# A transformer block's expert layer: results fetched beside the last quad's weights, the last quad's wide passes added by one-hot, the first quad's tokens gathered

## The chip, the cores and the metric

The program runs on one core of a Trainium2 chip. The time is the device time of one execution in microseconds (us), the median of several runs. Lower is better.

## The reference

Two transformer blocks run one after the other on 512 tokens of width 1024, all in fp32. The first ends with a mixture of experts, and only that part is changed:

```python
# t: 512 x 1024; 32 experts in 4 groups of 8; top 2 experts of one group per token
combine = sum(one_hot(expert_ids, 32) * w_top[..., None], axis=1)
for e in range(32):
    hid = silu(t @ w_gate[e]) * (t @ w_up[e])        # 1024 -> 256
    out = out + combine[:, e:e + 1] * (hid @ w_down[e])   # 256 -> 1024
x = x + gate2 * out
```

Every token picks a group, then two experts of it, so 1024 (token, expert) pairs are spread unevenly: with these inputs, one group takes most of them.

## The kernel before

The residual `x` is kept transposed (eight tiles `x[k]` of 128 features x 512 tokens). The expert layer (`moe`, from L1047) routes, then works through the experts in eight **quads**: quad q holds expert q of each of the four groups (`ex(q, c)` = 8c + q). Each expert has 32 slots in its quad's tile of 128 rows; what an expert has beyond 32 tokens goes through a **wide pass** of 128 rows (`more`, a runtime `If` on the expert's count, and `wide_pass`). In the traced run the second expert of each quad has such a pass, the other three skip theirs. A further block (L1446) for experts with more than 160 tokens is skipped whole.

Per quad: `expert1` (gate and up, 64 matmuls of 32-row strips, then tanh on ACT and products on DVE), `xpose` of the next quad's tokens (eight transposes, evictions by DVE and ACT in turns), `turn` (transpose of the hidden tile), `expert2` (down projection, 32 matmuls, scaled by ACT), `scatter` of the rows to a DRAM table `yd` by POOL; then the four `If`s with `load(6)` (six weight tiles of 512 KB on SP) and `gather_wide` (POOL, tokens of the wide passes from a DRAM copy `h2d`) after each.

How tokens reach a quad: `fill_table` scatters token numbers and weights to a DRAM table by eight POOL instructions, and ACT loads them back as slot tables (`slots0`, `slots[1]`). Quads 2 to 7 gather by `slots0`. Quads 0 and 1 come too early for that: `select` builds a one-hot `oh` (rank equals slot) and reads token number, weight and target row with 16 small matmuls against `val`. Quad 1 then gathers by that number; quad 0 uses the one-hot itself: `pick` multiplies it with the token tiles `xn` by 64 matmuls.

The last quad (`late` in `expert2`) isn't scattered: its rows are split in two fp32r parts `ys`, and `combine` adds them to `x` by one-hot matmuls, in two halves of 256 tokens. The other results come back from `yd`: `fetch(i)` loads two tiles of 128 rows on SP, `collect(i)` sums them on POOL, transposes, and adds to `x` on DVE. The order at the end:

```python
again = [self.mwt() for _ in range(6)]
...                                  # the block for over 160 tokens (L1446)
got = [fetch(i) for i in range(4)]
ys = expert2(NQ - 1, hT, *gat[NQ - 1][1:3])
for hf, hs in enumerate(HALVES):
    combine(ys, hs)
    for i in (2 * hf, 2 * hf + 1):
        collect(i, got[i])
```

The framework orders each engine's instructions within a stretch between two `If`s by its own estimate of when they are ready, program order deciding among the ready ones; an engine then runs its list strictly in order. `mwt()` hands out 30 weight buffers in rotation. Behind the layer, the second block enters (`enter`): sums of squares (ACT, POOL), four weight tiles split in two fp32r parts (`wsplit`, L257 on ACT, L258 on DVE), then a dense stream of matmuls to the end.

Of the kernel before, what the change touches and what calls it, by code (L numbers as in the profile page):

```python
# [205 lines left out]
class Net:  # L206
# [840 lines left out]
    def moe(self):  # L1047
# [37 lines left out]
        def sm(shape, tag):  # L1085
            return self.t(mp, shape, "r_" + tag)
# [74 lines left out]
        wa = sm([P, 4, NE], "wa")  # L1161
        outer(wa, o1)

        td = sm([P, 4, 2, 4], "td")
        tu = td.bitcast(U32)
        slot = sm([P, 4, NE], "slot")
# [9 lines left out]
        for a, sa in enumerate((s12, s2)):  # L1176
# [2 lines left out]
            v.tensor_scalar_add(tu[:, :, a, 1], tokb, BIG - 1.0 + a * S)  # L1179
            v.tensor_copy(td[:, :, a, 2:3], (w1, w2)[a])  # L1180
            v.tensor_scalar_add(td[:, :, a, 3], tokb, BIG)

        val = sm([P, 4, NE, 3], "val")
        v.tensor_copy(val[:, :, :, 0], tokb.unsqueeze(2).to_broadcast([P, 4, NE]))
        v.tensor_copy(val[:, :, :, 1], wa)
        v.scalar_tensor_tensor(val[:, :, :, 2], a2, float(S), tokb.unsqueeze(2).to_broadcast([P, 4, NE]), op0=ALU.mult, op1=ALU.add)


        q1, q2, q3, q4 = (self.t(self.tp, [P, S], "cy" if q < 2 else "th") for q in range(4))

# [26 lines left out]
        def select(q):  # L1217

            oh = self.t(mp, [P, 4, 4, first], "oh")
            for i in range(4):  # L1220
                v.tensor_tensor(oh[:, i], iota[:, :first].unsqueeze(1).to_broadcast([P, 4, first]),
                                rank[:, i, q::8].unsqueeze(2).to_broadcast([P, 4, first]), ALU.is_equal)
            pv = self.pst([P, 3], "mm")
            for i in range(4):
                for c in range(4):
                    cs = slice(32 * c, 32 * c + 32)
                    mm(pv[cs, :], oh[:, i, c, :], val[:, i, ex(q, c), :], start=i == 0, stop=i == 3, tile_position=(0, 32 * c))
            idx = self.t(mp, [P, 1], "idy", U32, bufs=2)
            v.tensor_scalar_add(idx, pv[:, 2:3], BIG - 1.0)
            wv = self.t(mp, [P, 1], "wv", bufs=2)  # L1230
            v.tensor_copy(wv, pv[:, 1:2])
            return oh, idx, wv, pv

        def fetch_tokens(xg, idu):
            g_.indirect_dma_start(out=xg, out_offset=None, in_=h2d, in_offset=bass.IndirectOffsetOnAxis(ap=idu, axis=0),
# [1 line left out]

        def gather(q):

            if q == 1:  # L1240
                _, idx, wv, pv = select(q)
                idu = self.t(mp, [P, 1], "idu", U32)
                v.tensor_scalar_add(idu, pv[:, 0:1], BIG - 1.0)
            else:
                at = slots0[:, q, :].bitcast(U32)
                idu, wv = at[:, 0:1], slots0[:, q, 2:3]
                idx = at[:, 1:2] if q < NQ - 1 else slots0[:, q, 3:4]
            fetch_tokens(xg, idu[:, 0:1])
            return xg, idx, wv

        def gather_wide(e, r=1):

            fetch_tokens(oxg[e // 8], slots[r][:, e, 0:1].bitcast(U32))

        def feed(xTs, hf, pt):

            for k in range(4):
                kk = 4 * hf + k
                if k % 2:
                    s.activation(xTs[hf][:, k, :], pt[:, k, :], AF.Identity, scale=self.gs2[:, kk:kk + 1], bias=mod[:, 3, kk:kk + 1])  # L1260
                else:
                    v.tensor_scalar(xTs[hf][:, k, :], pt[:, k, :], self.gs2[:, kk:kk + 1], mod[:, 3, kk:kk + 1], op0=ALU.mult, op1=ALU.add)

        def xtiles():
            return [self.t(mp, [P, 4, P], f"xgT{hf}") for hf in range(2)]
# [7 lines left out]
                feed(xTs, hf, pt)  # L1273
            return xTs

        def pick(oh):

            xTs = xtiles()
            for hf in range(2):
                pt = self.pst([P, 4, P], "mm")  # L1280
                for k in range(4):
                    kk = 4 * hf + k
                    for i in range(4):
                        mm(pt[:, k, :], xn[i][:, kk * P:(kk + 1) * P], oh[:, i].rearrange("p a b -> p (a b)"),
                           start=k + i == 0, stop=k + i == 6)
                feed(xTs, hf, pt)
            return xTs

        def glu(th, gate, up):

            s.activation(th, gate, AF.Tanh, scale=0.5)  # L1291
# [24 lines left out]
            g_.indirect_dma_start(out=yd, out_offset=bass.IndirectOffsetOnAxis(ap=idx, axis=0), in_=y,  # L1316
                                  in_offset=None, bounds_check=2 * S - 1, oob_is_err=False)

        def expert2(q, hT, idx, wv):

            late = q == NQ - 1
            ys = yt[:1]
            if late:
                ys = [self.t(mp, [P, D], f"ys{i}", F32R) for i in range(2)]
                ys.append(self.t(self.tp, [P, S], "sq", F32R))
                v.tensor_scalar(ys[-1], tokens, idx, None, op0=ALU.is_equal)
            for n in range(2):
                py = self.pst([P, S], "mm")
                ns = slice(n * S, (n + 1) * S)
                for k in range(2):  # L1330
                    for c in range(4):
                        cs = slice(32 * c, 32 * c + 32)
                        mm(py[cs, :], hT[:, k, cs], wt[ex(q, c), 4 + k][:, ns], start=k == 0, stop=k == 1, tile_position=(0, 32 * c))  # L1333
                s.activation(ys[0][:, ns], py, AF.Copy, scale=wv)
                if late:
                    v.scalar_tensor_tensor(ys[1][:, ns], py, wv, ys[0][:, ns], op0=ALU.mult, op1=ALU.subtract)
            if not late:
                scatter(ys[0], idx[:, 0:1])
            return ys

        def wide_pass(e, r, w):

            xT = xpose(oxg[e // 8], oxT)
            pt = None
            for a in range(2):
                ps = self.pst([P, 2, P], "mm")
                for k in range(KT):
                    mm(ps.rearrange("p a b -> p (a b)"), xT[k // 4][:, k % 4, :], piece(w, k)[:, 256 * a:256 * a + 256],
                       start=k == 0, stop=k == KT - 1)
                    if a and k == 4:  # L1350
                        pt = self.pst([P, P], "mm")
                        pe.transpose(pt, oth[:, 0, :], ident)
                        s.copy(ohT[:, 0, :], pt)
                glu(oth[:, a, :], ps[:, 0, :], ps[:, 1, :])
            py = [self.pst([P, S], "mm") for _ in range(2)]
            for k in range(2):
                if k:
                    pt = self.pst([P, P], "mm")
                    pe.transpose(pt, oth[:, 1, :], ident)
                    s.copy(ohT[:, 1, :], pt)  # L1360
                for n in range(2):
                    mm(py[n], ohT[:, k, :], w[4 + k][:, n * S:(n + 1) * S], start=k == 0, stop=k == 1)
            for n in range(2):
                s.activation(yt[1][:, n * S:(n + 1) * S], py[n], AF.Copy, scale=slots[r][:, e, 2:3])
            scatter(yt[1], slots[r][:, e, 1:2].bitcast(U32))

        def combine(ys, hs):
# [10 lines left out]
            for i in [ex(q, c) for c in range(4)]:  # L1378
                rvs[i] = nc.values_load(cmi[0:1, i:i + 1], min_val=0, max_val=S)

        def more(e):

            with tc.If(rvs[e] > first):
                wide_pass(e, 1, [wt[e, j] for j in range(6)])

        def rest(e, w, r=2):

# [6 lines left out]
                    wide_pass(e, r, w)  # L1394
                    rest(e, w, r + 1)

        def fetch(i):

            ys = [self.mwt() for _ in range(2)]
            for a in range(2):  # L1400
                nc.sync.dma_start(ys[a], yd[a * S + i * P:a * S + (i + 1) * P, :])
            return ys

        def collect(i, ys):
# [9 lines left out]
                    xs = self.x[kk][:, i * P:(i + 1) * P]  # L1414
                    v.scalar_tensor_tensor(xs, pt[:, k, :], mod[:, 5, kk:kk + 1], xs, op0=ALU.mult, op1=ALU.add)

        gat = {0: select(0)}
        xt = pick(gat[0][0])
        gat[1] = gather(1)
        fill_table()  # L1420
        count(0)
        for c in range(4):
            gather_wide(ex(0, c))
        for q in range(NQ):
            last = q == NQ - 1
            th = expert1(q, xt)

            if not last:
                with tc.issue_after(self.end1.ins):
                    xt = xpose(gat[q + 1][0])  # L1430
                count(q + 1)
            with tc.issue_after(self.end1.ins):
                hT = turn(th)
            if not last:
                if q + 2 < NQ:
                    gat[q + 2] = gather(q + 2)
                with tc.issue_after(self.turned.ins):
                    expert2(q, hT, *gat[q][1:3])
            for c in range(4):
                more(ex(q, c))  # L1440
                load(6)
                if not last:
                    gather_wide(ex(q + 1, c))
        again = [self.mwt() for _ in range(6)]
        top = nc.values_load(cmi[0:1, NE:NE + 1], min_val=0, max_val=S)
        with tc.If(top > first + wide):  # L1446
            for r in range(2, 5):
                wide_slots(g_, r)
            for e in range(NE):
                rvs[e] = nc.values_load(cmi[0:1, e:e + 1], min_val=0, max_val=S)  # L1450
                rest(e, again)
        got = [fetch(i) for i in range(4)]
        ys = expert2(NQ - 1, hT, *gat[NQ - 1][1:3])
        for hf, hs in enumerate(HALVES):
            combine(ys, hs)
            for i in (2 * hf, 2 * hf + 1):
                collect(i, got[i])
        for k in range(KT):
            self.save(f"x2_{k}", self.x[k])

# [512 lines left out]
```

## Time and profile before

| | us |
|---|---|
| median of 3 runs (range) | 2174.67 (2170.82 to 2176.73) |
| the profiled execution: its time | 2174.14 |
| its span, first to last instruction | 2172.3 |
| TensorE busy in the span | 2001.5 |
| mean granted TensorE clock | 0.974 |

The span is what the trace covers; its times count from its first instruction. TensorE (PE) is the matmul engine, with its weight loads on a row of their own (PEld); DVE, ACT and POOL are the vector, scalar and GpSimd engines; SP issues transfers. A "q" behind an engine (ACTq, PEq) is its sequencer, which also issues that engine's transfers. The expert layer lies between about 466 and 809 us of the span.

### The profile page before, as it was taken

The page shows a single profiled execution, that of the slowest core. Times are in us where ns is not written, and L with a number is a line of the kernel's source. Part 1 is how long each engine was busy: PE and PEld are TensorE (multiplying, and loading weights), DVE is VectorE, ACT ScalarE, POOL GpSimd, SP SyncE. Part 2 cuts the span into 40 slices and gives each one's busy share as a digit, 9 for nine tenths or more (in the row PEclk, how much of TensorE's full clock was granted, in tenths as well). Part 3 has the DMA queues.
Part 4 walks back from the last instruction along what each step waited for, and adds up shares of the span by engine and source line. Part 5 has one row for each costly group of instructions (what it writes and reads, how often), then busy time and mean ns, then how long its engine had stood idle before and what let it go on. Part 6 is the DMA issues. An engine that isn't in the chain of part 4 may idle for free. (4 is left out here: it accounts for less than half of the span.)

```text
span 2172.3 us, 32065 instructions
## 1 busy us (share of the span) xinstructions
PE 2001.5 (92%) x12818; PEld 1549.5 (71%) x12818; DVE 1030.4 (47%) x1889; ACT 703.1 (32%) x1173; POOL 218.6 (10%) x243
## 2 busy tenths in 40 slices
PE   5999999778787769999999999999999999999996
PEld 3677767554434348888888788888878888888885
DVE  4763664641111046552455674645664457542443
ACT  3532343122222123322233352524543243322231
POOL 3020002012121121000003200000000041000002
PEclk9999999889999989999999999999999999999998
DMA  8443215366999943333333132423233322333321
GB/s 268 118 137 109 88 52 182 129 241 208 359 394 375 342 172 102 97 90 104 97 97 98 56 100 78 117 65 106 68 104 91 111 68 88 97 95 100 97 88 39
DMA packets 110620, 294.81 MB, mean 136 GB/s; under 512 B 20023, under 2 KB 31415, under 8 KB 110444
## 3 DMA queue, kind: packets, MB, share of 16 engines
q1 hardware_dynamic: 99676, 275.98, 38.9%
q0 software_dynamic: 9856, 14.29, 2.1%
q8 instruction: 113, 1.85, 0.3%
q10 hardware_dynamic: 912, 2.18, 0.3%
q14 instruction: 63, 0.52, 0.1%
HBM read 296.20 MB, written 18.43 MB: 145 GB/s over the span
## 5 line engine op out<-in xcount | busy, mean ns | idle before, releaser
L274 PE MATMUL mm<-xh,wh 128*128 128x512 f32 (+1 forms) x1584 | 615.1, 390 | 10.2 <-ACT wh L257 6.1
L275 PE MATMUL mm<-xl,wh 128*128 128x512 f32 (+1 forms) x1584 | 604.6, 382 | 5.4 <-DVE xl L1578 5.3
L276 PE MATMUL mm<-xh,wl 128*128 128x512 f32 (+1 forms) x1584 | 601.4, 380 | 0.0
L257 ACT ACTIVATE wh<-wraw 128x1024 fp32r<-128x1024 f32 (+3 forms) x282 | 274.1, 974 | 735.7 <-PE mm L275 647.0
L258 DVE TENSOR_TENSOR wl<-wraw,wh 128x1024 fp32r<-128x1024 f32 (+3 forms) x282 | 315.0, 1118 | 192.0 <-ACT wh L257 190.3
L274 PEld LDWEIGHTS mm<-xh,wh 128*128 128x128 f32 x1584 | 301.2, 191 | 76.6 <-ACT wh L257 8.1
L275 PEld LDWEIGHTS mm<-xl,wh 128*128 128x128 f32 x1584 | 302.7, 191 | 60.9 <-DVE xl L1578 7.0
L276 PEld LDWEIGHTS mm<-xh,wl 128*128 128x128 f32 x1584 | 301.6, 190 | 56.8 <-issue 2.0
L340 POOL TENSOR_TENSOR ss<-ss,sq 128x256 f32<-128x256 f32 (+1 forms) x69 | 65.4, 947 | 919.1 <-ACT sq L339 917.4
L274 PE MATMUL mm<-hh,wh 128*128 128x512 f32 (+1 forms) x416 | 148.5, 357 | 0.0
L276 PE MATMUL mm<-hh,wl 128*128 128x512 f32 (+1 forms) x416 | 148.3, 357 | 0.0
L275 PE MATMUL mm<-hl,wh 128*128 128x512 f32 (+1 forms) x416 | 148.2, 356 | 0.0
L1301 PE MATMUL mm<-wmoe,xgT 128*32 128x512 f32 x512 | 68.9, 624 | 21.7 <-DMA wmoe<-in_wmoe 11.6
L276 PEld LDWEIGHTS mm<-hh,wl 128*128 128x128 f32 x416 | 78.6, 189 | 11.3
L274 PEld LDWEIGHTS mm<-hh,wh 128*128 128x128 f32 x416 | 78.6, 189 | 11.3
L275 PEld LDWEIGHTS mm<-hl,wh 128*128 128x128 f32 x416 | 78.6, 189 | 11.3
L1638 DVE TENSOR_TENSOR sq<-mm,rsb 128x512 f32<-128x512 f32 x44 | 30.4, 691 | 104.0 <-PE mm L276 103.8
L1333 PE MATMUL mm<-wmoe,hT 128*32 128x512 f32 x256 | 51.9, 624 | 24.9 <-DMA wmoe<-in_wmoe 14.2
L1633 DVE TENSOR_TENSOR cy<-mm,rsb 128x512 f32<-128x512 f32 x44 | 30.4, 690 | 85.4 <-PE mm L276 83.5
L1301 PEld LDWEIGHTS mm<-wmoe,xgT 128*32 128x32 f32 x512 | 20.5, 114 | 67.9 <-issue 34.0
L1292 DVE SCALAR_TENSOR_TENSOR mth<-mth,mm 128x256 f32<-128x256 f32 x8 | 3.4, 420 | 114.5 <-ACT mth L1291 88.7
L1333 PEld LDWEIGHTS mm<-wmoe,hT 128*32 128x32 f32 x256 | 11.8, 113 | 60.2 <-issue 29.0
(510 smaller groups left out, 2587.0 us busy)
## 6 DMA issues: line engine op xcount, KB each, us to landing
wmoe<-in_wmoe SPq DMA_DIRECT2D x192, 512.0 KB
wraw<-in_win SPq DMA_DIRECT2D x90, 512.0 KB
wraw<-in_wgu SPq DMA_DIRECT2D x88, 512.0 KB
wraw<-in_wada SPq DMA_DIRECT2D x32, 512.0 KB
wraw<-in_wd SPq DMA_DIRECT2D x32, 448.0 KB
big<-in_wada SPq DMA_DIRECT2D x16, 512.0 KB
wraw<-in_wd SPq DMA_DIRECT2D x16, 512.0 KB
wraw<-in_wout SPq DMA_DIRECT2D x16, 256.0 KB
```

Of the source, the lines that this page charges most:

```text
L257: self.nc.scalar.activation(h[:, :n], raw[:, :n], AF.Copy)
L258: self.nc.vector.tensor_sub(l[:, :n], raw[:, :n], h[:, :n])
L274: mm(ps, w1, xh[k], start=start and i == 0, stop=False)
L275: mm(ps, w1, xl[k], start=False, stop=False)
L276: mm(ps, w2, xh[k], start=False, stop=stop and i == nk - 1)
L340: self.nc.gpsimd.tensor_add(acc[:, hs], acc[:, hs], sq[:, hs])
L1292: v.scalar_tensor_tensor(th, th, 1.0, gate, op0=ALU.add, op1=ALU.mult)
L1301: self.end1 = mm(ps[cs].rearrange("p a b c -> p (a b c)"), xT[k // 4][:, k % 4, cs], piece(ws[c], k), start=k == 0, stop=k == KT - 1, tile ...
L1333: mm(py[cs, :], hT[:, k, cs], wt[ex(q, c), 4 + k][:, ns], start=k == 0, stop=k == 1, tile_position=(0, 32 * c))
L1633: v.tensor_mul(t1, pp[0], rb)
L1638: v.tensor_mul(t2, pp[1], rb)
```

## The change

Four things, in the order of the diff. The lines that build `val` move up, ahead of those that build the table's rows. Quad 0's tokens come by a gather from `h2d`, as quad 1's do, and `pick` is gone. In the last quad the wide passes, too, are split in two parts and added to `x` by one-hot (`parts`, `places`, and `combine` over all 512 tokens, inside the `If`), so no result of the last quad goes to `yd`. And the end is reordered: the skipped block of L1446 and the fetch of three of the four pieces, now on ACT's queue, stand ahead of the last quad's `expert1`; behind its `If`s come the collects (the fourth fetch into the tiles of the first), then `expert2` and `combine`.

```diff
@@ routing: the three lines of val, unchanged, now ahead of td / slot / rows
         def gather(q):
-            if q == 1:
-                _, idx, wv, pv = select(q)
-                idu = self.t(mp, [P, 1], "idu", U32)
+            if q < 2:
+                idx, wv, pv = select(q)
+                idu = self.t(mp, [P, 1], "idu", U32, bufs=2)
...
-        def pick(oh):
-            xTs = xtiles()
-            for hf in range(2):
...
+        def parts(py, wv, ys, ns):
+            s.activation(ys[0][:, ns], py, AF.Copy, scale=wv)
+            v.scalar_tensor_tensor(ys[1][:, ns], py, wv, ys[0][:, ns], op0=ALU.mult, op1=ALU.subtract)
+
+        def places(ys, idx):
+            v.tensor_scalar(ys[2], tokens, idx, None, op0=ALU.is_equal)
...
+        def wide_pass(e, r, w, late=None):
...
+            wv = slots[r][:, e, 2:3]
+            if late:
+                places(late, slots[r][:, e, 3:4])
             for n in range(2):
-                s.activation(yt[1][:, n * S:(n + 1) * S], py[n], AF.Copy, scale=slots[r][:, e, 2:3])
+                ns = slice(n * S, (n + 1) * S)
+                if late:
+                    parts(py[n], wv, late, ns)
+                else:
+                    s.activation(yt[1][:, ns], py[n], AF.Copy, scale=wv)
+            if late:
+                return combine(late, slice(0, S))
             scatter(yt[1], slots[r][:, e, 1:2].bitcast(U32))
...
-        def fetch(i):
-            ys = [self.mwt() for _ in range(2)]
+        def fetch(i, ys):
             for a in range(2):
-                nc.sync.dma_start(ys[a], yd[a * S + i * P:a * S + (i + 1) * P, :])
+                nc.scalar.dma_start(ys[a], yd[a * S + i * P:a * S + (i + 1) * P, :])
...
-        gat = {0: select(0)}
-        xt = pick(gat[0][0])
+        gat = {0: gather(0)}
+        xt = xpose(gat[0][0])
         gat[1] = gather(1)
         fill_table()
...
-        for q in range(NQ):
+        for q in range(NQ - 1):
...
-        again = [self.mwt() for _ in range(6)]
+        spare = [self.mwt() for _ in range(6)]
         top = nc.values_load(cmi[0:1, NE:NE + 1], min_val=0, max_val=S)
         with tc.If(top > first + wide):
...
-        got = [fetch(i) for i in range(4)]
-        ys = expert2(NQ - 1, hT, *gat[NQ - 1][1:3])
-        for hf, hs in enumerate(HALVES):
-            combine(ys, hs)
-            for i in (2 * hf, 2 * hf + 1):
-                collect(i, got[i])
+        q = NQ - 1
+        got = [fetch(i, spare[2 * i:2 * i + 2]) for i in range(3)]
+        count(q)
+        th = expert1(q, xt)
+        with tc.issue_after(self.end1.ins):
+            hT = turn(th)
+        late = [self.t(mp, [P, D], f"ys{i}", F32R) for i in range(2)]
+        late.append(self.t(self.tp, [P, S], "sq", F32R))
+        for c in range(4):
+            more(ex(q, c), late)
+        for i in range(4):
+            collect(i, got[i])
+            if i == 0:
+                got.append(fetch(3, got[0]))
+        expert2(q, hT, *gat[q][1:3], late)
+        for hs in HALVES:
+            combine(late, hs)
```

## Rows read from the trace of the kernel before

**Rows 1.** Stage table: busy us (instructions) by engine, clock, DMA share, GB/s

```profile
545.00:745.00 200.00, 160.59 (x850) 77.69 (x850) 27.52 (x78) 45.63 (x102) 36.02 (x36) 0.98 0.96 368
...
818.00:2172.30 1354.30, 1319.31 (x6568) 1110.09 (x6568) 695.53 (x1076) 462.49 (x677) 84.29 (x101) 0.99 0.30 90
```

**Rows 2.** Timeline of the head, all engines: start, duration, instruction

```profile
481.37 1.08 POOL L1208 DMA_INDIRECT tab<-r_td,r_rows  x1 [60.54 <-DVE r_td L1180]
...
486.42 0.16 DVE L1229 TENSOR_SCALAR idy<-mm 128x1 uint32<-128x1 f32 x1 [4.21 <-remote]
...
490.45 0.97 POOL L1208 DMA_INDIRECT tab<-r_td,r_rows  x1 [0.30 <-issue]
...
494.96 0.46 ACT L1260 ACTIVATE xgT<-mm,mod,gs 128x128 f32<-128x128 f32 x1 [16.66 <-DMA slots<-tab]
...
501.28 0.99 POOL L1235 DMA_INDIRECT xg<-h2d,idu  x1 [0.30 <-issue]
...
507.42 0.38 ACT L1291 ACTIVATE mth<-mm 128x256 f32<-128x256 f32 x1 [9.73 <-PE mm L1301]
```

**Rows 3.** Timeline of TensorE around the last quad

```profile
745.20 1.06 PE L1301 MATMUL mm<-wmoe,xgT 128*32 128x512 f32 x6 [1.23 <-PEq L1383]
752.53 9.27 PE L1301 MATMUL mm<-wmoe,xgT 128*32 128x512 f32 x58 [6.27 <-DMA wmoe<-in_wmoe]
...
775.50 1.98 PE L1362 MATMUL mm<-wmoe,rsb 128*128 128x512 f32 x4 [0.41 <-ACT rsb L1360]
784.76 5.10 PE L1333 MATMUL mm<-wmoe,hT 128*32 128x512 f32 x32 [7.28 <-PEq L1446]
```

**Rows 4.** Timeline of SP and POOL around the last quad

```profile
744.00 13.55 SPq L1045 DMA_DIRECT2D wmoe<-in_wmoe  x14
788.74 3.84 SPq L1401 DMA_DIRECT2D wmoe<-yd  x8
...
753.45 0.99 POOL L1235 DMA_INDIRECT htok<-h2d,slots  x1 [0.30 <-issue]
...
793.77 2.33 POOL L1407 TENSOR_TENSOR wmoe<-wmoe,wmoe 128x1024 f32<-128x1024 f32 x1 [14.23 <-DMA wmoe<-yd]
```

**Rows 5.** Timeline of DVE, then TensorE, behind the last quad

```profile
789.06 0.75 DVE L1336 SCALAR_TENSOR_TENSOR ys<-mm,slots,ys 128x512 fp32r<-128x512 f32 x1 [14.85 <-ACT ys L1334]
...
791.39 2.82 DVE L1373 SCALAR_TENSOR_TENSOR x<-mm,mod,x 128x256 f32<-128x256 f32 x7
...
805.24 4.21 DVE L1415 SCALAR_TENSOR_TENSOR x<-mm,mod,x 128x128 f32<-128x128 f32 x16
...
818.05 0.58 PE L275 MATMUL mm<-xl,wh 128*128 128x256 f32 x1 [1.55 <-DVE xl L1578]
```

**Rows 6.** Windows around quad 1's gather and the last weights

```profile
503.00:505.00 2.00, 1.47 (x7) 0.34 (x10) 0.00 (x0) 0.00 (x0) 0.56 (x1) 1.00 0.58 152
...
758.00:766.00 8.00, 5.30 (x41) 1.90 (x33) 1.30 (x4) 0.76 (x2) 0.00 (x0) 1.00 0.98 386
```

**Rows 7.** DMA queues in 736 to 738: packets, MB, share of 16 engines

```profile
q1 hardware_dynamic: 128, 0.46, 62.3%
q0 software_dynamic: 100, 0.32, 39.4%
```

**Rows 8.** Timeline of TensorE in quad 1

```profile
528.65 7.85 PE L1301 MATMUL mm<-wmoe,xgT 128*32 128x512 f32 x64 [1.31 <-PEq L1383]
536.44 1.09 PE L1272 MATMUL mm<-c_ident,xg 128*128 128x128 f32 x8
```

**Rows 9.** Sequencer instructions of L1446 and L1383: duration ns min/median/max, starts

```profile
L1446 PEldq COMPARE_BRANCH  x1: 4263/4263/4263, 779.9 to 779.9; - x1
...
L1446 POOLq INC_SWDGE_SEM  x1: 1718/1718/1718, 786.8 to 786.8; - x1
...
L1383 PEldq COMPARE_BRANCH  x40: 70/212/1173, 511.6 to 778.1; - x40
```

**Rows 10.** Waits of SP's queue, 460 to 830: us in all, times, longest

```profile
SPq L1045 <- DMA wmoe<-in_wmoe: 68.9, 63, 2.0
```

More of the change, by code (lines that the diff above doesn't have):

```diff
@@ L1162, in moe @@
         outer(wa, o1)
+        val = sm([P, 4, NE, 3], "val")
+        v.tensor_copy(val[:, :, :, 0], tokb.unsqueeze(2).to_broadcast([P, 4, NE]))
+        v.tensor_copy(val[:, :, :, 1], wa)
+        v.scalar_tensor_tensor(val[:, :, :, 2], a2, float(S), tokb.unsqueeze(2).to_broadcast([P, 4, NE]), op0=ALU.mult, op1=ALU.add)
         td = sm([P, 4, 2, 4], "td")
@@ L1181, in moe @@
             v.tensor_scalar_add(td[:, :, a, 3], tokb, BIG)
[L1183 to L1186, printed above, removed]
         q1, q2, q3, q4 = (self.t(self.tp, [P, S], "cy" if q < 2 else "th") for q in range(4))
@@ L1231, in select @@
             v.tensor_copy(wv, pv[:, 1:2])
-            return oh, idx, wv, pv
+            return idx, wv, pv
         def fetch_tokens(xg, idu):
@@ L1272, in xpose @@
                     pe.transpose(pt[:, k, :], xg[:, (4 * hf + k) * P:(4 * hf + k + 1) * P], ident)
-                feed(xTs, hf, pt)
-            return xTs
-        def pick(oh):
-            xTs = xtiles()
-            for hf in range(2):
[L1280 to L1285, printed above, removed]
                 feed(xTs, hf, pt)
@@ L1317, in scatter, with expert2 @@
                                   in_offset=None, bounds_check=2 * S - 1, oob_is_err=False)
-        def expert2(q, hT, idx, wv):
-            late = q == NQ - 1
-            ys = yt[:1]
+        def parts(py, wv, ys, ns):
[3 more added lines that the diff above has]
+            v.tensor_scalar(ys[2], tokens, idx, None, op0=ALU.is_equal)
+        def expert2(q, hT, idx, wv, late=None):
             if late:
-                ys = [self.t(mp, [P, D], f"ys{i}", F32R) for i in range(2)]
-                ys.append(self.t(self.tp, [P, S], "sq", F32R))
-                v.tensor_scalar(ys[-1], tokens, idx, None, op0=ALU.is_equal)
+                places(late, idx)
             for n in range(2):
@@ L1333, in expert2 @@
                         mm(py[cs, :], hT[:, k, cs], wt[ex(q, c), 4 + k][:, ns], start=k == 0, stop=k == 1, tile_position=(0, 32 * c))
-                s.activation(ys[0][:, ns], py, AF.Copy, scale=wv)
                 if late:
-                    v.scalar_tensor_tensor(ys[1][:, ns], py, wv, ys[0][:, ns], op0=ALU.mult, op1=ALU.subtract)
+                    parts(py, wv, late, ns)
+                else:
+                    s.activation(yt[0][:, ns], py, AF.Copy, scale=wv)
             if not late:
-                scatter(ys[0], idx[:, 0:1])
-            return ys
-        def wide_pass(e, r, w):
+                scatter(yt[0], idx[:, 0:1])
+        def wide_pass(e, r, w, late=None):
             xT = xpose(oxg[e // 8], oxT)
@@ L1362, in wide_pass @@
                     mm(py[n], ohT[:, k, :], w[4 + k][:, n * S:(n + 1) * S], start=k == 0, stop=k == 1)
+            wv = slots[r][:, e, 2:3]
+            if late:
+                places(late, slots[r][:, e, 3:4])
             for n in range(2):
-                s.activation(yt[1][:, n * S:(n + 1) * S], py[n], AF.Copy, scale=slots[r][:, e, 2:3])
+                ns = slice(n * S, (n + 1) * S)
+                if late:
+                    parts(py[n], wv, late, ns)
+                else:
+                    s.activation(yt[1][:, ns], py[n], AF.Copy, scale=wv)
+            if late:
+                return combine(late, slice(0, S))
             scatter(yt[1], slots[r][:, e, 1:2].bitcast(U32))
@@ L1379, in count, with more @@
                 rvs[i] = nc.values_load(cmi[0:1, i:i + 1], min_val=0, max_val=S)
-        def more(e):
+        def more(e, late=None):
             with tc.If(rvs[e] > first):
-                wide_pass(e, 1, [wt[e, j] for j in range(6)])
+                wide_pass(e, 1, [wt[e, j] for j in range(6)], late)
         def rest(e, w, r=2):
@@ L1423, in moe @@
             gather_wide(ex(0, c))
-        for q in range(NQ):
-            last = q == NQ - 1
+        for q in range(NQ - 1):
             th = expert1(q, xt)
[L1428 to L1431, printed above, removed]
+            with tc.issue_after(self.end1.ins):
+                xt = xpose(gat[q + 1][0])
+            count(q + 1)
             with tc.issue_after(self.end1.ins):
                 hT = turn(th)
[L1434 to L1438, printed above, removed]
+            if q + 2 < NQ:
+                gat[q + 2] = gather(q + 2)
+            with tc.issue_after(self.turned.ins):
+                expert2(q, hT, *gat[q][1:3])
             for c in range(4):
@@ L1441, in moe @@
                 load(6)
-                if not last:
-                    gather_wide(ex(q + 1, c))
-        again = [self.mwt() for _ in range(6)]
+                gather_wide(ex(q + 1, c))
+        spare = [self.mwt() for _ in range(6)]
         top = nc.values_load(cmi[0:1, NE:NE + 1], min_val=0, max_val=S)
@@ L1450, in moe @@
                 rvs[e] = nc.values_load(cmi[0:1, e:e + 1], min_val=0, max_val=S)
-                rest(e, again)
-        got = [fetch(i) for i in range(4)]
-        ys = expert2(NQ - 1, hT, *gat[NQ - 1][1:3])
-        for hf, hs in enumerate(HALVES):
-            combine(ys, hs)
-            for i in (2 * hf, 2 * hf + 1):
-                collect(i, got[i])
+                rest(e, spare)
+        q = NQ - 1
+        got = [fetch(i, spare[2 * i:2 * i + 2]) for i in range(3)]
+        count(q)
+        th = expert1(q, xt)
+        with tc.issue_after(self.end1.ins):
+            hT = turn(th)
[10 more added lines that the diff above has]
+            combine(late, hs)
         for k in range(KT):
```

## The prediction, made before the changed kernel was run

> **What bounds the kernel now.** I read the stage table first: 818 to 2172.3 us is a matmul stream that the change doesn't touch, TensorE busy in 1319 of 1354 us, so a microsecond won before 818 should arrive at the end. From 545 to 745 us (six expert quads) the DMA share is 0.96: weights and TensorE drive each other, since the loads of the next quad wait for buffers that the wide pass frees. A quad that starts earlier frees its buffers earlier, so I carry a gain of the first quad 1:1 [rows 1].
>
> Then the two ends. **Head:** the one-hot of quad 0 is consumed by 64 matmuls (`pick`), whose results DVE and ACT evict in turns. ACT stood 16.66 us in its queue behind the small loads of the slot tables, which wait for POOL's eight table scatters (481.37 to 491.42); it evicted only at 494.96. The tanh of quad 0 comes at 507.42 [rows 2]. **Tail:** quad 7's gate and up matmuls end at 761.80, the last wide pass at 777.48; TensorE then sits 7.28 us behind the test of L1446, does the last down projection (784.76 to 789.86), and waits for results, which SP begins to fetch only at 788.74 [rows 3, 4]. DVE writes the last x at 809.45, and the steady stream begins at 818.05 [rows 5].
>
> **Head, step by step.** Selection is unchanged: its 16 matmuls end where DVE reads them, 486.42 [rows 2]. The moved `val` lines change nothing: their inputs are late, not their place. One more DVE cast (0.16), and the token numbers are ready at about 486.8. The gather is one POOL instruction, 0.99 us. Its landing isn't shown for quad 0; the nearest is the gather of quad 1, issued at 501.28, with traffic until 505 at the latest: 3.7 us on nearly idle engines [rows 2, 6]. While weights stream it shares: in 736 to 738 POOL's queue had 39% of the engines beside SP's 62% [rows 7]; that could double it. I take 4.2: 491.0. Eight transposes 1.09 us [rows 8], with evictions behind them (half a microsecond each, DVE and ACT in turns), let the first matmul start about 492.5. The 64 gate and up matmuls of a quad take 7.85 [rows 8]; in quad 0, quad 1's selection stood among them, which now fits ahead, while TensorE waits for the gather. So the tanh comes at 492.5 + 7.9 = 500.4; I take 501: **-6.5 us**. Bounds: -8 (landing in 3 us), and 0, if POOL takes the gather after the scatters (issue 491.7, landing 495.4, start 497) with quad 1's selection back in the way, or if ACT's evictions stay behind the slot loads. A gather among the scatters delays these: it waits for 486.8 where the third scatter stood at 484, and takes a place of 1.3, so some 4 us; the slot loads follow, and then quad 0's wide gather, which stood two places of 1.3 ahead of quad 1's at 501.28: now near 502.7, landed by 506.4. The wide pass reads it 7.3 us after the tanh, at 508.3. Hidden by 2 us; without that cover it would cost what is lacking.
>
> **Tail, what moves ahead.** The skipped L1446 block goes before quad 7's gate and up matmuls. On TensorE its branch lasts 4.26 us [rows 9]: 745 to 749.5, where TensorE did six matmuls and then waited for weights until 752.53 [rows 3]. Cost 0; without that wait, 4.3. On POOL the branch and its 1.72 us counter instruction [rows 9] come after the gathers issued until 754.44 [rows 4], and the counter must follow their landing: 3.7 to 7.4 us from the last issue, by the two prices above, 757 to 761; I take 761, as weights stream [rows 6], and 762.7 with the counter. The fetch waits for that counter, as SP did before: it ended at 788.5, and SP issued at 788.74 [rows 4, 9].
>
> **The new wait.** The six fetch issues now stand in ACT's queue ahead of quad 7's tanh, ready at 761.8; behind it wait DVE, the turn, and the whole wide pass. Besides the counter, an issue can wait for an earlier transfer: SP's loads did so 63 times, and 14 issues took 13.55 us, where eight fetches on SP took 3.84 [rows 4, 10]. Weights stream until 766 [rows 6], so the later issues fall among the last loads. Lower bound: from 762.7 six issues of 0.45: 765.4, +3.6. Upper: the sixth waits for the last load, and weights run at half rate from 763.7 (fetch traffic one us behind its issue): 763.7 + 2 x 2.6 + 0.5 = 769.4, +7.6. I take 766.8: **+5.0 us**. That ACT had slot loads ahead of evictions [rows 2] says that its queue isn't rearranged when a wait turns out long; if the tanh stands first after all, it is 0. The down weights, last in the stream, are used only at the wide pass's end, more than 10 us later: 0.
>
> **Tail, what is left behind the wide pass**, from its last matmul (777.48 then). Before: last x at +31.97, stream at +40.6 [rows 3, 5]. After, inside the pass: two parts on DVE at 0.75, eight full-width adds at no more than 0.75 (128x512 out of PSUM takes 0.75; two half-width adds 0.80) [rows 5]: +7.6. Leaving the branch and two skipped tests: 1.23 [rows 3]; I take 1.3. Then DVE has 32 collect adds at 0.26 (8.4), two parts (1.5), 16 half-width adds at 0.40 (6.4) [rows 5], and 1 us of bubbles: +26.2, so -5.8. GpSimd's sums of the first three fetches end during the wide pass (data from 764 to 775, 2.33 us each [rows 4]), and the down projection (5.1) runs under DVE's collects. The fourth fetch goes into the first one's tile after collect 0: issue at about +9.8, its sum begins 5.0 us later (788.74 to 793.77 [rows 4]), 2.3 to add, 1 to transpose: +18, while DVE has other work until +24. Hidden; past that it would cost 1:1. Between last x and stream there were 8.6 us, in which ACT and DVE split four weights; these can come earlier, since SP has no fetches in front: 0 to 2.7; I take 1.2. Sum **-7.0 us** (-5 to -9).
>
> **Sum:** -6.5 + 5.0 - 7.0 = -8.5 us. The profiled execution took 2174.14 (span 2172.3 and 1.8 around it), 0.5 under the median shown: 2165.6 for it, **2166.2** in terms of the median.
>
> **Rivals.** *Fetch and weights in lockstep:* ACT's queue, +7.6 instead of 5.0: 2168.8, and up to 2170 where POOL's counter comes later. For it, the shares [rows 7]; against it, only the last of six issues fall among the last loads. The Trainium skill says so too (DMA: Bandwidth & Descriptors, section Issuing engines are not separate DMA queues): transfers of all issuing engines run on the same 16 engines and interleave, so a second queue saves issue time alone. The trace agrees (62% beside 39%); by that rule the fetch's 3.1 MB are added to a full stream, some 8 us at 386 GB/s.
>
> *The head gives nothing*, by either order named above: 2172.7. For it, the order that ACT took before; against it, the gather's inputs are ready 4 us before the last scatter is issued.
>
> *The down projection stands behind the fourth collect on TensorE:* 5.0 + 2.3 + 1 less the 2 us that collects 1 and 2 fill, +6.3: 2172.5. Against it: its operands are ready long before.
>
> *The tanh stands ahead of the fetch:* no +5.0: 2161.2.
>
> *Slower: the skipped late passes cost a far branch each.* Their bodies grow by 16 matmuls and eight adds. TensorE's branches over today's bodies took 0.21 us in the median, 1.17 at most, that over L1446 4.26 [rows 9]. If the three skips of quad 7 cost 4.26 each, that is 3 x 4.05 = +12.2: 2178.4, slower than before; it decides from 2.8 us a skip. Against it: 16 matmuls are little beside the 50 in a body now. The Trainium skill has the mechanism (Runtime: NRT & Kernel Launch, section Instruction fetch mechanics): a taken branch whose target isn't in the engine's two-page window stalls while that page is fetched. The 4.26 us fit it; by that rule the skips stall only if a body outgrows the window, which none did so far.
>
> **Chances and range.** Forecast 0.46 (own range 2162 to 2169.5: head -8 to -5, wait +3.6 to +7, tail -5 to -9); lockstep 0.13; nothing from the head 0.20; tanh first 0.08; down projection late 0.07; far branches 0.06. The range of 8 in 10 leaves out the far branches and about half of "tanh first", where the other terms are good too, and the rest for unknown: 2159 to 2177. A measurement of this kernel can tell 0.3%, 6.5 us, from no change. Under 2168.1 lie four fifths of the forecast (0.37), tanh first (0.08) and a part of lockstep and head (0.05): faster 0.50. Over 2181.2 only far branches with more on top, and the unknown: 0.06. Between: 0.44.
>
> **What would show it.** Right: quad 0's tanh at 500 to 502; its gather among the scatters on POOL; six fetch issues on ACT's queue ending at 765 to 768, quad 7's tanh right behind; the down projection under DVE's collects; the stream some 34 us behind the last wide matmul. Wrong: ACT's first eviction still behind the slot loads; quad 7's tanh ahead of the fetch, or past 770; skips over 2.8 us; TensorE waiting for GpSimd before the last down projection. The forecast fails most easily in the head, since the order that POOL and ACT will have there stands in no row.

## The result, and the profile after

The changed kernel takes 2189.17 us in the median (5 runs, 2185.63 to 2190.45), the kernel before 2175.66 beside it: ratio 1.0061, 95% interval 1.0049 to 1.0072. It is slower by 13.5 us where 8.5 us less were forecast. Its profiled span is 2186.3 against 2172.3.

The start of the expert layer wanders from trace to trace for reasons outside the change, so the stretches are counted from the routing's first add (L1102). Three rows of the kernel before that the rows above don't hold, from its timeline: that add, and the tanh of quads 6 and 7.

```profile
469.12 0.31 DVE L1102 TENSOR_TENSOR r_L<-sm,r 128x144 f32<-128x144 f32 x1
...
719.10 0.39 ACT L1291 ACTIVATE mth<-mm 128x256 f32<-128x256 f32 x1 [8.75 <-PE mm L1301]
...
761.84 0.38 ACT L1291 ACTIVATE mth<-mm 128x256 f32<-128x256 f32 x1 [17.08 <-PE mm L1301]
```

| stretch, us | before | after | differs | forecast |
|---|---|---|---|---|
| routing's add to quad 0's tanh | 38.30 | 37.05 | -1.25 | -6.5 |
| to quad 6's tanh | 211.68 | 213.08 | +1.4 | 0 |
| to quad 7's tanh | 42.74 | 55.82 | +13.1 | +5.0 |
| to the end of the last wide matmul | 15.64 | 18.84 | +3.2 | 0 |
| to the end of the last add to x | 31.97 | 30.70 | -1.3 | -5.8 |
| to the end of the span | 1362.85 | 1361.52 | -1.3 | -1.2 |

The head of the changed kernel, timeline of all engines (answers to [rows 2]):

```profile
469.29 0.31 DVE L1102 TENSOR_TENSOR r_L<-sm,r 128x144 f32<-128x144 f32 x1
...
482.53 0.60 PE L1227 MATMUL mm<-r_val,oh 128*32 128x3 f32 x32 [5.17 <-DVE r_val L1166]
...
489.37 0.97 POOL L1208 DMA_INDIRECT tab<-r_td,r_rows  x1 [0.30 <-issue]
...
489.49 0.16 DVE L1229 TENSOR_SCALAR idy<-mm 128x1 uint32<-128x1 f32 x1 [7.11 <-issue]
...
490.64 1.06 POOL L1235 DMA_INDIRECT xg<-h2d,idu  x1 [0.30 <-issue]
...
494.96 1.94 PE L1272 MATMUL mm<-c_ident,xg 128*128 128x128 f32 x8 [11.83 <-DMA xg<-h2d,idu]
...
496.59 0.46 ACT L1260 ACTIVATE xgT<-mm,mod,gs 128x128 f32<-128x128 f32 x1 [17.95 <-DMA slots<-tab]
...
506.34 0.39 ACT L1278 ACTIVATE mth<-mm 128x256 f32<-128x256 f32 x1 [7.56 <-PE mm L1288]
```

The gather goes out as the eighth of POOL's nine instructions (490.64, the scatter of 489.37 just before it), not among the first scatters, and ACT's first eviction still ends a wait on the slot loads.

Its last quad, timeline of all engines (answers to [rows 3, 4]):

```profile
719.42 0.38 ACT L1278 ACTIVATE mth<-mm 128x256 f32<-128x256 f32 x1 [8.96 <-PE mm L1288]
...
752.76 9.23 PE L1288 MATMUL mm<-wmoe,xgT 128*32 128x512 f32 x64 [8.80 <-ACTq L1443]
...
764.38 10.80 ACTq L1401 DMA_DIRECT2D wmoe<-yd  x7
...
772.50 2.33 POOL L1407 TENSOR_TENSOR wmoe<-wmoe,wmoe 128x1024 f32<-128x1024 f32 x1 [18.34 <-DMA wmoe<-yd]
...
775.24 0.38 ACT L1278 ACTIVATE mth<-mm 128x256 f32<-128x256 f32 x1 [30.49 <-DMA wmoe<-yd]
...
777.77 2.63 DVE L1313 TENSOR_SCALAR sq<-c_iota,slots 128x512 fp32r<-128x512 f32 x1 [1.24 <-PEq L1384]
...
777.77 2.35 POOL L1407 TENSOR_TENSOR wmoe<-wmoe,wmoe 128x1024 f32<-128x1024 f32 x1 [0.43 <-PEq L1384]
...
780.78 4.23 PE L1340 MATMUL mm<-wmoe,cy 128*128 128x256 f32 x10 [0.44 <-DVE cy L1262]
...
792.10 1.98 PE L1354 MATMUL mm<-wmoe,rsb 128*128 128x512 f32 x4 [0.41 <-ACT rsb L1352]
```

ACT's queue has **seven** fetch issues ahead of quad 7's tanh, not six, and they last until 775.18. The gate and up matmuls had ended at 761.99. The profile puts the wait down to the fetched data; the row to look at is POOL's: its first sum ends at 774.83, and the last of the seven issues follows at once, at 774.86 (the row above has all seven merged). Three fetches make six issues, so the seventh is half of the fourth; the other half leaves at 803.78, behind the collects. With the fourth fetch on SP's queue, below, the row has six.

In ACT's instruction list the seventh writes the second tile of the first fetch. The fourth fetch goes into the first one's tiles: the second of them is free as soon as GpSimd has added it, while the first is read by `collect(0)`. So this half of the fourth fetch, which the code has behind four `If`s and `collect(0)`, was placed ahead of them all, and there it waits for GpSimd.

Behind the last wide matmul, timeline of DVE, POOL and TensorE (answers to [rows 5]):

```profile
795.57 5.35 DVE L1374 SCALAR_TENSOR_TENSOR x<-mm,mod,x 128x512 f32<-128x512 f32 x8
...
802.93 6.29 DVE L1415 SCALAR_TENSOR_TENSOR x<-mm,mod,x 128x128 f32<-128x128 f32 x24 [0.42 <-PE mm L1411]
...
807.14 2.35 POOL L1407 TENSOR_TENSOR wmoe<-wmoe,wmoe 128x1024 f32<-128x1024 f32 x1 [27.02 <-DMA wmoe<-yd]
...
809.55 1.97 PE L1411 MATMUL mm<-c_ident,wmoe 128*128 128x128 f32 x8 [3.41 <-POOL wmoe L1407]
811.44 5.47 PE L1325 MATMUL mm<-wmoe,hT 128*32 128x512 f32 x32
...
818.43 6.35 DVE L1374 SCALAR_TENSOR_TENSOR x<-mm,mod,x 128x256 f32<-128x256 f32 x16
```

The down projection stands behind the fourth collect's transposes, and these wait for GpSimd's fourth sum.

### The profile page after: what moved, and what is told of

It reads as the page before. It is cut to its first block, busy times and chain, and to the rows that moved or that the text cites. A ratio compares the mean times of both kernels' runs of the same rounds, so it can differ in the third digit from the quotient of the medians.

```text
span 2186.3 us, 32032 instructions
## 1 busy us (share of the span) xinstructions
PE 1999.4 (91%) x12778; PEld 1544.6 (71%) x12778; DVE 1041.4 (48%) x1901; ACT 702.8 (32%) x1173; POOL 220.0 (10%) x243
## 5 line engine op out<-in xcount | busy, mean ns | idle before, releaser
L276 PEld LDWEIGHTS mm<-hh,wl 128*128 128x128 f32 x416 | 78.6, 189 | 11.2
```

What stands on the lines that cost most here:

```text
L276: mm(ps, w2, xh[k], start=False, stop=stop and i == nk - 1)
```

## The experiments

**Two theories.** The queue's order: a few instructions stand behind ones that wait for something else, on ACT (the tanh), on TensorE (the down projection) and on POOL (the gather). Against it, transfers in lockstep: 3.1 MB of results are added to the weight stream, and the last quad pays for them wherever they are issued.

**All fetch issues on SP's queue**

```diff
-                nc.scalar.dma_start(ys[a], yd[a * S + i * P:a * S + (i + 1) * P, :])
+                nc.sync.dma_start(ys[a], yd[a * S + i * P:a * S + (i + 1) * P, :])
```

> All eight fetch issues on SP's queue, the rest as in the changed kernel. Theory (ACT's queue): in the changed kernel seven fetch issues stand ahead of quad 7's tanh, and the last of them, the second half of the fourth fetch, waits for GpSimd's first sum (772.50 + 2.33); off ACT, the tanh comes back from 775.24 to about 762, the wide pass runs without the 14 us pause before it, and the time falls by 14 to 16 us: 2173 to 2176. Rival (lockstep of transfers): 3.1 MB are added to the weight stream wherever they are issued, the tanh comes at 762, but the wide pass waits for its down weights some 8 us: its last matmul ends at 785 to 787, and the time falls by 6 to 9 us only: 2180 to 2183.

2172.4 us; ratio to before 0.9981 (0.997 to 0.9991). Timeline of all engines:

```profile
766.53 0.38 ACT L1278 ACTIVATE mth<-mm 128x256 f32<-128x256 f32 x1 [18.29 <-PE mm L1288]
...
769.05 0.49 DVE L1313 TENSOR_SCALAR sq<-c_iota,slots 128x512 fp32r<-128x512 f32 x1 [1.24 <-DMA wmoe<-in_wmoe]
...
769.07 23.31 SPq L1401 DMA_DIRECT2D wmoe<-yd  x8
...
770.85 2.43 PE L1340 MATMUL mm<-wmoe,cy 128*128 128x256 f32 x10
...
777.04 2.35 POOL L1407 TENSOR_TENSOR wmoe<-wmoe,wmoe 128x1024 f32<-128x1024 f32 x1 [19.42 <-DMA wmoe<-yd]
```

The gain of 16.8 us is a little more than the 14 to 16 expected. Quad 7's tanh follows that of quad 6 by 44.17 us (before 42.74, after 55.82), and the wide pass takes 15.82 from there (before 15.64).

Lockstep falls too, but not by this run alone: here the two streams hardly meet, since the first fetch is issued at 769.07, when the weights' queue had come down to 31% of the engines (769 to 770). In the changed kernel and in the next run (only the fourth fetch on SP's queue) they do meet: from 766 to 768 of the next run the results have 46.8% of the engines and the weights 45.4%. Yet in neither does a row of TensorE's wide pass wait for a transfer. Whether the overlap made the six issues longer (3.4 us in the changed kernel, 5.3 in the next run) isn't shown.

With the 14 us pause of TensorE goes the cold clock: from 776 to 782 of the changed kernel, where its wide pass begins behind that pause, the granted clock is 0.50 (1.2 GHz); from 762 to 776 of this run, which holds the end of the gate and up matmuls and the first half of the wide pass, it is 1.00 (2.4). Stage table of the changed kernel (columns as in [rows 1]):

```profile
776.00:782.00 6.00, 3.83 (x13) 2.90 (x14) 4.46 (x7) 1.42 (x4) 3.69 (x2) 0.50 0.27 94
```

Stage table of this run:

```profile
762.00:776.00 14.00, 11.11 (x72) 7.48 (x65) 3.54 (x9) 2.75 (x7) 0.00 (x0) 1.00 0.90 325
```

**Only the fourth fetch on SP's queue**

```diff
-                got.append(fetch(3, got[0]))
+                got.append(fetch(3, got[0], nc.sync))
```

> Only the two issues of the fourth fetch go to SP's queue; the six others stay on ACT's, ahead of the tanh. Theory (the seventh issue): the six are issued by 767.75 as in the changed kernel, the tanh follows at once, at about 768 instead of 775.24, and the time falls by 7 to 10 us: 2179 to 2182. Rival (the six issues themselves, or the transfers, hold the chain): the tanh or the wide pass stays within 2 us of where it was: 2187 to 2189.

2182.8 us (ratio 1.0025, 1.0014 to 1.0037). Timeline of ACT:

```profile
765.35 5.31 ACTq L1401 DMA_DIRECT2D wmoe<-yd  x6
770.70 0.38 ACT L1278 ACTIVATE mth<-mm 128x256 f32<-128x256 f32 x1 [24.84 <-DMA wmoe<-yd]
```

The tanh follows the sixth issue at once, 51.01 after quad 6's. Against the run with all on SP that leaves +6.8 us for the six issues, and the seventh alone cost 55.82 - 51.01 = 4.8. The theory had the tanh at 768: it missed that the six start at 765.35, 2.9 us after the gate and up matmuls end, and take 5.3 us here. The median, 6.4 less than the changed kernel's, lies just outside the 7 to 10 expected. The wide pass takes 17.24 here, with the granted clock still at 0.50 from 772 to 776.

**The last down projection ahead of the fourth collect**

```diff
-        for i in range(4):
+        for i in range(3):
             collect(i, got[i])
...
         expert2(q, hT, *gat[q][1:3], late)
-        for hs in HALVES:
-            combine(late, hs)
+        combine(late, HALVES[0])
+        collect(3, got[3])
+        combine(late, HALVES[1])
```

> The last down projection and the first half of its adds ahead of the fourth collect. Theory (order on TensorE): the down projection no longer waits for the fourth fetch's sum; DVE has 24 collect adds, 2 parts, 8 adds, 8 collect adds and 8 adds in a row, and the last x comes 4 to 5.5 us sooner after the last wide matmul than the 30.7 us of the changed kernel: 2184 to 2185. Rival (DVE's own work sets the end there): no more than 1 us: 2188 to 2189.

2184.73 us (1.0036, 1.0025 to 1.0046). Timeline of TensorE and DVE:

```profile
797.76 1.98 PE L1354 MATMUL mm<-wmoe,rsb 128*128 128x512 f32 x4 [0.41 <-ACT rsb L1352]
...
811.54 3.64 PE L1325 MATMUL mm<-wmoe,hT 128*32 128x512 f32 x32
...
821.89 3.21 DVE L1374 SCALAR_TENSOR_TENSOR x<-mm,mod,x 128x256 f32<-128x256 f32 x8
```

From the end of the last wide matmul (799.74) to the last x (825.10) it is 25.36 instead of 30.70: the 5.3 us are the down projection's place, as the theory had it.

**Quad 0 made late** (on the kernel before; the first two picks are done for nothing)

```diff
-        xt = pick(gat[0][0])
+        for _ in range(3):
+            xt = pick(gat[0][0])
```

> The kernel before with the 64 matmuls that pick quad 0's tokens, and their evictions, done three times over, the first two results unused: the first quad is late by about 10 to 14 us, the rest is untouched. Theory 1:1: quad 7's tanh is late by as much as quad 0's, within 1.5 us, and so is the end: 2186 to 2190. Rival (the quads in between have slack, since weights pace them): less than half of it arrives at quad 7: under 2182.

2188.77 us (1.005, 1.0033 to 1.0067). Timeline of DVE and ACT:

```profile
469.46 0.31 DVE L1102 TENSOR_TENSOR r_L<-sm,r 128x144 f32<-128x144 f32 x1
...
519.60 0.38 ACT L1291 ACTIVATE mth<-mm 128x256 f32<-128x256 f32 x1 [7.14 <-PE mm L1301]
...
773.37 0.38 ACT L1291 ACTIVATE mth<-mm 128x256 f32<-128x256 f32 x1 [16.86 <-PE mm L1301]
```

Quad 0's tanh is 11.8 us late (50.14 from the add), quad 7's 11.2, the end of the span 10.5. A delay of the head arrives almost whole.

**Both repairs together**: the diff of the first experiment and that of the down projection.

> Both repairs: all fetch issues on SP's queue, and the last down projection with the first half of its adds ahead of the fourth collect. Theory (two separate causes on one chain): the gains add. From 2172.4 with the fetch on SP, 5.3 us fewer between the last wide matmul and the last x, and about 1.5 after it, as the run with the other order of the down projection showed: 2165 to 2167, faster than before by 0.4%. Rival: with the wide pass 12 us earlier the fourth fetch's sum is late for the fourth collect again, and half of it is lost: 2169 or more.

2169.25 us, before 2175.88: ratio 0.9972 (0.9961 to 0.9982), the lowest median of the study, though the two runs below don't differ from it beyond the noise. Timeline of TensorE and DVE:

```profile
778.88 1.98 PE L1354 MATMUL mm<-wmoe,rsb 128*128 128x512 f32 x4 [0.41 <-ACT rsb L1352]
...
793.87 3.64 PE L1325 MATMUL mm<-wmoe,hT 128*32 128x512 f32 x32
...
804.22 3.22 DVE L1374 SCALAR_TENSOR_TENSOR x<-mm,mod,x 128x256 f32<-128x256 f32 x8
```

The expectation, 2165 to 2167, was missed: the median shows 3.2 of some 7. From the last wide matmul (end 780.86) to the last x it is 26.58: 3.3 us less than with the fetch on SP alone (29.86), of 5.3 expected. The time lies in the rival's range, but not for its reason: the fourth collect's transposes don't wait here. The traces show the other 2.0 us. The fetch on SP had already won 0.8 of this stretch (29.86 for 30.70). And the 24 transposes of the first three collects take 5.35 here, with a granted clock of 0.52 from 788 to 794, but 4.13 in the run with the other order alone (0.68 from 807 to 812), each time after 3.39 us of idle time; so the down projection starts 13.0 us after the last wide matmul instead of 11.8. The 1.5 us behind the last x, counted from one trace, didn't come: 1361.06 from there to the end of the span, 1361.19 with the fetch on SP.

**The same with the old head** (`select` returns `oh` again, and `pick` is back)

```diff
-        gat = {0: gather(0)}
-        xt = xpose(gat[0][0])
+        gat = {0: select(0)}
+        xt = pick(gat[0][0])
```

> As the run with both repairs, but with the head of the kernel before: quad 0 by the 64 matmuls on its one-hot, no gather. Theory (the gather's place): measured from the routing's first add, quad 0's tanh comes at 38.3 us with the old head and at 37.1 with the new one, since the gather stands behind seven table scatters and ACT's eviction still behind the slot loads; 1 us is all that the head is worth: 0 to 2 us slower than the run with both repairs. Rival (the forecast's head): the end is 5 to 7 us later.

2170.06 us (0.9976, 0.9967 to 0.9985): no different from 2169.25. Timeline of DVE and ACT:

```profile
473.07 0.31 DVE L1102 TENSOR_TENSOR r_L<-sm,r 128x144 f32<-128x144 f32 x1
...
509.31 0.38 ACT L1291 ACTIVATE mth<-mm 128x256 f32<-128x256 f32 x1 [7.50 <-PE mm L1301]
```

The old head takes 36.24 us here and 38.30 in the kernel before; the new one 36.98 to 37.71 in the five traces that have it as the change left it. The gather is worth nothing that these runs can show.

**The same with the head's order by hand** (new head; the last three scatters tied behind the gather, the slot loads behind quad 0's evictions):

```diff
+                    with tc.issue_after(first_fetch.ins) if 2 * i + a > 4 else nullcontext():
                         t = g_.indirect_dma_start(out=self.tab, ...
+            with tc.issue_after(last_fed.ins):
                 for c in range(4):
                     nc.scalar.dma_start(slots0[32 * c:32 * c + 32], tab[:first, 8 * c:8 * c + 8])
```

> As the run with both repairs, with the order of the head given by hand: the last three table scatters behind quad 0's gather on GpSimd, and the slot loads behind quad 0's evictions on ACT. Theory (the order in the head costs): ACT's first eviction no longer waits 1.5 us behind the slot loads, the gather goes out as soon as its numbers are there, and quad 0's tanh comes 2 to 3 us earlier after the routing's first add (34 to 35 instead of 37.1); the end follows: 2 to 3 us. Rival (the selection's result, read 7 us after its matmuls, is what the gather waits for): the gather moves by less than 1 us, and the end by 1 to 2.

2169.93 us (0.9973, 0.996 to 0.9986). Timeline of all engines:

```profile
469.09 0.31 DVE L1102 TENSOR_TENSOR r_L<-sm,r 128x144 f32<-128x144 f32 x1
...
489.69 1.06 POOL L1237 DMA_INDIRECT xg<-h2d,idu  x1 [2.10 <-issue]
...
495.63 0.46 ACT L1262 ACTIVATE xgT<-mm,mod,gs 128x128 f32<-128x128 f32 x1 [17.22 <-DVE xgT L1264]
...
503.80 1.00 POOL L1237 DMA_INDIRECT htok<-h2d,slots  x1 [4.83 <-DMA slots<-tab]
504.12 0.38 ACT L1280 ACTIVATE mth<-mm 128x256 f32<-128x256 f32 x1 [6.16 <-PE mm L1290]
...
507.74 5.34 PE L1327 MATMUL mm<-wmoe,hT 128*32 128x512 f32 x32 [0.64 <-ACT hT L1301]
...
514.06 1.06 PE L1274 MATMUL mm<-c_ident,htok 128*128 128x128 f32 x8 [0.99 <-ACTq L1386]
```

Quad 0's tanh comes 35.03 after the add, as expected; the end doesn't follow. Quad 1's tanh has only 0.6 us left of the gain (66.59 from the add against 67.19 with both repairs). The slot tables are later in exchange, and quad 0's wide gathers leave from 503.80 on, after 4.83 us of waiting for them; but the profile puts the wait of the wide pass (514.06) down to the `If`'s test, not to the gather. Most of the gain is gone before that: quad 0's down projection takes 5.34 us here, at a granted clock of 0.50 from 508 to 510, and 3.64 with both repairs (1.00 from 512 to 514); it ends 43.99 after the add here, 44.50 there and 43.81 in the changed kernel. TensorE was busy for 1.8 us in the 4 before 508 here, and for 2.2 in the 4 before 512 there. What made the clock fall no run isolated.

## Why the prediction was wrong

- **Head, -6.5: wrong.** The step that failed is "the token numbers are ready at about 486.8. The gather is one POOL instruction", with POOL free to take it. The numbers were read at 489.49, and the list had seven scatters ahead of it: issue 490.64. (The prediction let the selection's matmuls end where DVE reads them; in the trace before they end at 482.97, and DVE reads 3.4 us later, 6.4 in the changed kernel.) Its landing, taken as 4.2 us, was nearly right (4.3: 494.96). ACT's evictions stayed behind the slot loads and the matmuls ran cold (granted clock 0.50 from 494 to 498); of 6.5 us 1.25 were left. So the rival in which the head gives nothing came true, and the run with the old head bears it out. The +1.4 in the quads 1 to 6 says little: in the five traces with this head quad 6's tanh comes 249.27 to 252.01 after the add, 249.98 before. That a gain of the head is carried 1:1 was right for a delay (11.2 of 11.8); for a gain it isn't shown: the one run that had one lost most of it in quad 0's down projection.
- **Block ahead of quad 7: nearly right.** It cost no wait behind weights, but TensorE's branch took 6.24 us, not 4.26, and the block released it 8.80 us after the wide pass, when the weights were there (752.53 in [rows 3]); the six matmuls that had fitted in the wait no longer do. In the changed kernel itself that costs nothing: the gate and up matmuls end 42.57 us after quad 6's tanh, 42.70 before. In the traces with the fetch off ACT the stretch to the tanh is 1.4 us longer than before (44.17 to 42.74) and 0.7 (43.45, both repairs).
- **The new wait, +5.0: the largest miss, +13.1.** For "the six fetch issues" the step was sized about right: +6.8, inside the bounds. What it left out is the seventh. The prediction placed the fourth fetch "after collect 0", from the order of the code; a transfer into a tile that is used again is ready when that tile's last reader is, and was placed by that, in front of the tanh: 4.8 us more there. Lockstep, the rival nearest to it, was wrong in its cause.
- **The wide pass, 0 forecast: +3.2.** TensorE had stood 14 us and ran it at the lower clock (ten matmuls 4.23 us, 2.43 with the fetch on SP), behind a one-hot of 2.63 us. Both go with the wait (15.82).
- **Behind the wide pass, -5.8 to the last x: -1.3.** The terms are right: eight full-width adds at 0.67, skips of 1.1 (1.3 taken), fourth fetch 9.7 us after the last wide matmul (9.8 taken). The step that failed is the place of the down projection "under DVE's collects": the rival with it behind the fourth collect came true and cost 5.3 us (6.3 forecast). In its right place the stretch is 25.36 to 26.58 (26.2 forecast).
- **After the last x, -1.2: right in size (-1.3), but by luck.** The forecast's reason was that the four weights can be split earlier. They came later: their loads leave SP from 817.02 on, 7.8 us before the last x (15.8 before), and ACT's first split begins at 828.25, 3.5 us after it (0.5 before). What the trace shows in its place: DVE's splits of x now stand ahead of its splits of the weights, where the steady stream had waited for one of x at 818.05 [rows 5]. That this gives the 1.3 isn't shown.
- **The far branches stayed away.** Leaving the pass and the two skips behind it cost DVE 1.1 us; TensorE's longest branch there took 2.09 us (1.17 was the longest before), under the 2.8 that would have decided.

Three of the four signs that the prediction named against itself stand in the trace: ACT's first eviction behind the slot loads, quad 7's tanh past 770, TensorE waiting for GpSimd ahead of the last down projection.

## What to carry to other kernels

When transfers are moved to another engine's queue, list what stands behind each issue there, and every issue that the same edit creates, also those that the code has much later: a reused tile makes a transfer ready long before its line is reached. Put transfers that can wait on a queue with nothing urgent behind them, here SP's: that one line was worth 16.8 us. And a sum of stretches is only as good as the order it assumes; where a planner sets the order, read the instruction list before sizing the terms.

## What the hardware showed unexpectedly

- The one-hot `sq` on DVE took 2.63 us when it began with GpSimd's sum of two SBUF tiles (777.77, 2.35 us), 0.49 where none ran beside it; DVE's adds out of PSUM beside the sum of 807.14 kept their 0.26. The Trainium skill (SBUF — State Buffer, section SBUF: two separate sides) says that the two engines share a port pair which one of them holds for a whole instruction; the 2.63 are 2.35 and 0.28 more, which fits. The trace of the run with the other order of the down projection has the same pair (2.63 beside 2.35).
- The selection's 32 tiny matmuls began at 482.53, and DVE got their result at 489.49, with nothing on TensorE behind them; in [rows 2], with `pick` behind them, at 486.42. Over all traces it is 6.3 to 7.7 us from the first matmul to DVE's reading without `pick`, and 4.1 to 4.8 with it. Why is open; no run isolated it.
